# Gate weights loaded ahead, square roots of both scan directions taken together, and the latents' squares moved from PSUM to SBUF

## The chip, the cores and the metric

One core of a Trainium2 chip runs the whole program. The metric is the device time of one execution in microseconds; less is better. In the text, PE is the matrix engine, DVE the vector engine, ACT the scalar engine, POOL the GpSimd engine and SP the queue from which all transfers are issued.

## The reference, cut to what matters

One encoder layer on 1024 tokens of width 1024, in float32. The part that the change touches is the first sub-layer, before attention:

```python
proj = rms_norm(x, attn_norm) @ w_in          # [x-branch 512 | gate branch 512 | latents 416]
for d in (forward, backward):
    xd = depthwise_conv(xr, conv_w[d], conv_b[d])         # four taps
    r = sigmoid(block_diag(xd, w_a[d]) + b_a[d])
    i = sigmoid(block_diag(xd, w_i[d]) + b_i[d])
    log_a = -8 * r * softplus(-lam[d]);  a = exp(log_a)
    h[d] = scan(a, sqrt(-expm1(2 * log_a)) * (i * xd))    # h_t = a_t h_(t-1) + b_t
lru_out = (h[0] + h[1]) * gelu(yg)
c_q, c_kv = rms_norm(latents[:256]), rms_norm(latents[256:384])
```

Latent attention (8 heads), an output projection, a cross-attention into 256 memory rows and a SwiGLU network with a width-3 convolution follow; they are written as before.

## The kernel before

The kernel is one straight program without loops at run time. A scheduler builds the order of each engine's instructions from the program's order and from its own estimate of times; each engine then runs its list in that order and waits where an operand or a buffer isn't ready. So an instruction that waits holds back everything behind it on the same engine.

Activations are kept as two parts, high and low, so that each product of the projections is three matmuls (`mm3`, issued in `mm`, L108). The weights are split in the same way by POOL: `whi` (L133) and `wlo` (L134), from a raw tile with two buffers into tiles of a pool with 12 buffers.

The first sub-layer works on four blocks `j` of 128 channels:

- `xr_stage(j)` projects the x-branch into a two-bank PSUM tile `psin` (48 matmuls), ACT writes the first tap for each direction (L347), and DVE adds three taps for each direction out of PSUM (L349, L351), into `xf`. The PSUM tile is free after the last tap. There are two such two-bank tiles (`pb2`), which `psin`, `y_stage` and `latents` take in turn.
- `y_stage(j)` projects the gate branch (48 matmuls) and computes its GeLU: Square and Tanh on ACT (L358, L360), two steps on DVE (L359, L361), the last of which frees the PSUM tile.
- `lru_stage(j)` does, for each direction, four gate matmuls `psg` into one-bank tiles (`pb1`, four of them), Tanh of them on ACT into `thr` and `thi` (L380), Exp into `av` (L383), Tanh and Sqrt of `thr` (L384, L385), on DVE `(av+1)*thr` (L387) and `(thi+1)*xf` (L388), their product on POOL (L389; on DVE in the last block) and the scan on DVE (L392 forward, L394 backward). Then the directions are added (L396) and gated (L398). Sqrt is in another function table of ACT than Exp and Tanh, so that the scheduler's list has ACT_TABLE_LOAD before and after it.

`latents(t)` projects the 416 latent columns for 128 tokens into another two-bank tile `pslat` (24 matmuls), ACT copies them out (L421) and sums their squares (L424, L425). The squares themselves are of no use; they are written into the unused second bank of `pslat`. POOL and DVE then scale the rows (L426 to L429), PE transposes them (`psc`, L615), and the products `pk` and `pq` follow. `mem_rows` squares the memory rows (L598) and transposes them (`psm`, L605).

`rope_tables` uses a tile `rtt` with the tag "yt" and one buffer, the same as that of `y_stage`; its two Sin (L479, L480) need a third function table. `gate_unit` clears a weight tile on POOL and loads it with eight small transfers; `addrows` loads the parameter rows that become the columns `pcols`.

Of the kernel before, what the change touches and what calls it, by code (L numbers as in the profile page):

```python
# [11 lines left out]
F32 = mybir.dt.float32  # L12
F32R = mybir.dt.float32r
I32 = mybir.dt.int32
AF = mybir.ActivationFunctionType
ALU = mybir.AluOpType
# [3 lines left out]
S = 1024  # L20
D = 1024
P = 128
# [3 lines left out]
NJ = LRU // P  # L26
# [6 lines left out]
QL = 256  # L33
# [50 lines left out]
def trunk_layer(ctx: ExitStack, tc: tile.TileContext, a: dict, out: bass.AP):  # L84
    nc = tc.nc
    act, dve, pool, pe = nc.scalar, nc.vector, nc.gpsimd, nc.tensor
# [7 lines left out]
    wp = abcd.enter_context(tc.tile_pool(name="wp", bufs=12, reuse_waits="tile"))  # L94
# [9 lines left out]
    def f(t):  # L104
        return t.bitcast(F32)

    def mm(ps, l, r, start, stop):
        return pe.matmul(ps, lhsT=l, rhs=r, start=start, stop=stop)  # L108

    def mm3(ps, lh, ll, rh, rl, start, stop):  # L110
        mm(ps, lh, rh, start, False)
        mm(ps, lh, rl, False, False)
        return mm(ps, ll, rh, False, stop)
# [48 lines left out]
    tp = ab.enter_context(tc.tile_pool(name="tp", bufs=2, reuse_waits="tile"))  # L162
# [4 lines left out]
    for t in range(NT):  # L167
        xt = tp.tile([P, D], F32, tag=("xf", "xf", "th0", "th0", "th1", "th1", "th1", "a")[t],
                     bufs=4 if 4 <= t < 7 else 2, name="xt")
# [11 lines left out]
    for t in range(NT):  # L181
# [10 lines left out]
        h, o = t // 4, (t % 4) * P  # L192
        for q in range(2):
            ps = pb1.tile([P, 512], F32, tag="b1", name="psx")
# [4 lines left out]
            act.activation(hT[h][0][:, q * 4:q * 4 + 4, o:o + P], pv, AF.Copy)  # L199
            last_lo = dve.tensor_sub(hT[h][1][:, q * 4:q * 4 + 4, o:o + P], pv, f(hT[h][0])[:, q * 4:q * 4 + 4, o:o + P])  # L200


    RR = tp.tile([P, 6, P], F32, tag="xr", bufs=2, name="RR")
    R1, R2, R3 = RR[:, 0], RR[:, 1], RR[:, 2]
# [89 lines left out]
    sp2 = const.tile([P, 8], F32, name="sp2")  # L294
# [14 lines left out]
        return ps  # L309

    lru = lrup.tile([P, NJ, S], F32, tag="lru", name="lru")
    wg = {}

    def gate_unit(jj):

        w = wp.tile([P, 1024], F32, tag="w", name="wgate")
        pool.memset(w, 0.0)
        rv = w.rearrange("p (j d g c) -> p j d g c", j=2, d=2, g=2)
        for b in range(2):
            for gi, nm in enumerate(("lru_w_a", "lru_w_i")):  # L320
                for d in range(2):
                    nc.sync.dma_start(
                        rv[64 * b:64 * b + 64, :, d, gi, 64 * b:64 * b + 64],
                        a[nm][0, d].rearrange("(j b) p c -> b p j c", b=2)[b][:, 2 * jj:2 * jj + 2, :])
        wg[jj] = w

    ssl = const.tile([P, NT], F32, name="ssl")
    ssm = const.tile([P, NT], F32, name="ssm")
    krss = bc.tile([P, NT], F32, name="krss")
# [11 lines left out]
    def xr_stage(j):  # L341

        ps = in_proj(j * P)
        xfs = [tp.tile([P, S], F32, tag=("xf", "xr")[j % 2], bufs=2, name="xf") for _ in range(2)]
        cw = [[col("conv_w", (d * 4 + k) * 4 + j) for k in range(4)] for d in range(2)]
        for d in range(2):
            act.activation(xfs[d], ps, AF.Identity, bias=col("conv_b", d * 4 + j), scale=cw[d][3 - 3 * d])  # L347
        for n in range(1, 4):
            dve.scalar_tensor_tensor(xfs[0][:, n:], ps[:, :S - n], cw[0][3 - n], xfs[0][:, n:], ALU.mult, ALU.add)  # L349
        for n in range(1, 4):  # L350
            dve.scalar_tensor_tensor(xfs[1][:, :S - n], ps[:, n:], cw[1][n], xfs[1][:, :S - n], ALU.mult, ALU.add)  # L351
        return xfs
# [8 lines left out]
        dve.scalar_tensor_tensor(y, t, 1.0, ps, ALU.add, ALU.mult)  # L361

    def lru_stage(j, xfs):
        hs = []
        for d in range(2):
            i = d * 4 + j
            xf = xfs[d]
            pss = []
            for h in range(2):
                for g in range(2):  # L370
                    ps = pb1.tile([P, 512], F32, tag="b1", name="psg")
                    wo = ((j % 2) * 4 + d * 2 + g) * P
                    sl = slice(h * 512, (h + 1) * 512)
                    mm(ps, wg[j // 2][:, wo:wo + P], xf[:, sl], True, True)
                    pss.append(ps)
            thr = tp.tile([P, S], F32, tag="th0", name="thr")
            thi = tp.tile([P, S], F32, tag="th1", bufs=4, name="thi")
            for h in range(2):
                for g in range(2):
                    act.activation((thr, thi)[g][:, h * 512:(h + 1) * 512], pss[h * 2 + g], AF.Tanh,  # L380
                                   bias=hb[:, g * 8 + i:g * 8 + i + 1], scale=0.5)
            av = tp.tile([P, S], F32, tag="a", name="av")
            act.activation(av, thr, AF.Exp, bias=sp4[:, 8 + i:9 + i], scale=sp4[:, 8 + i:9 + i])  # L383
            act.activation(thr, thr, AF.Tanh, bias=sp2[:, i:i + 1], scale=sp2[:, i:i + 1])  # L384
            act.activation(thr, thr, AF.Sqrt, scale=0.25)  # L385
            m = thr
            dve.scalar_tensor_tensor(m, av, 1.0, thr, ALU.add, ALU.mult)  # L387
            dve.scalar_tensor_tensor(thi, thi, 1.0, xf, ALU.add, ALU.mult)  # L388
            (dve if j == NJ - 1 else pool).tensor_mul(thi, thi, m)  # L389
            h = thi  # L390
            if d == 0:
                dve.tensor_tensor_scan(h, av, thi, 0.0, ALU.mult, ALU.add)  # L392
            else:
                dve.tensor_tensor_scan(h[:, ::-1], av[:, ::-1], thi[:, ::-1], 0.0, ALU.mult, ALU.add)  # L394
            hs.append(h)
        dve.tensor_add(hs[0], hs[0], hs[1])  # L396
        y = lru[:, j, :]
        dve.scalar_tensor_tensor(y, hs[0], 0.5, y, ALU.mult, ALU.mult)  # L398
# [10 lines left out]

    cns = sm.tile([P, NT, LAT], F32, tag="cns", bufs=1, name="cns")  # L410

    def latents(t):
        h, o = t // 4, (t % 4) * P
        ps = pb2.tile([P, S], F32, tag="b2", name="pslat")
        for k in range(KD):
            wh, wl = wl_[k // 2]
            c = (k % 2) * LAT
            mm3(ps[:, :LAT], hT[h][0][:, k, o:o + P], hT[h][1][:, k, o:o + P],
                wh[:, c:c + LAT], wl[:, c:c + LAT], k == 0, k == KD - 1)
        cn = cns[:, t]  # L420
        act.activation(cn, ps[:, :LAT], AF.Copy)  # L421
        s2 = sm.tile([P, 2], F32, tag="s2", name="s2")
        junk = ps[:, 512:512 + QL]
        act.activation(junk, cn[:, :QL], AF.Square, scale=QL ** -0.5, accum_out=s2[:, 0:1])  # L424
        act.activation(junk[:, :KVL], cn[:, QL:QL + KVL], AF.Square, scale=KVL ** -0.5, accum_out=s2[:, 1:2])  # L425
        pool.tensor_scalar(s2, s2, EPS, 1.0, ALU.add, ALU.mult)  # L426
        pool.tensor_tensor(s2, s2, nhalf[:, :2], ALU.pow)
        dve.tensor_scalar(cn[:, :QL], cn[:, :QL], s2[:, 0:1], None, ALU.mult)
        dve.tensor_scalar(cn[:, QL:QL + KVL], cn[:, QL:QL + KVL], s2[:, 1:2], None, ALU.mult)  # L429
# [72 lines left out]

    xrs = {0: xr_stage(0)}
    xrs[1] = xr_stage(1)
    gate_unit(0)
    rC, rS = rope_tables()
    y_stage(0)
    lru_stage(0, xrs[0])
    xrs[2] = xr_stage(2)
    y_stage(1)  # L510
    gate_unit(1)
    lru_stage(1, xrs[1])
    xrs[3] = xr_stage(3)
    y_stage(2)
    lru_stage(2, xrs[2])
    y_stage(3)
    lru_stage(3, xrs[3])
    lat_units()
    for t in range(NT):
        latents(t)  # L520
# [293 lines left out]
    for s in range(NQ + 2):  # L814
        H, i = divmod(s, NT)
# [45 lines left out]
    def w_out_unit(half, kk):  # L861
        g = "lru_g" if kk < 2 else "mla_g"
        return wunit(lambda raw: pairs(raw, a["w_out"][0, kk * 2 * P:(kk + 1) * 2 * P, half * 512:(half + 1) * 512]),
                     1024, [col(g, (kk % 2) * 2), col(g, (kk % 2) * 2 + 1)], "ad")
# [66 lines left out]
    wo = [w_out_unit(0, kk) for kk in range(2)]  # L931
# [11 lines left out]
    with tc.issue_after(x2_load.ins):  # L943
        wo = [w_out_unit(1, kk) for kk in range(4)]
# [265 lines left out]
```

## Time and profile before

| | us |
|---|---|
| median of 3 runs | 1464.61 (1464.01 to 1468.86) |
| the profiled execution | 1464.37 |
| its span | 1462.3 |
| outside the span | 2.07 |
| PE busy in the span | 1405.3 (96%) |
| DVE, POOL, ACT busy | 866.1, 570.4, 545.8 |
| mean granted clock of PE | 0.993 |

All times in the text are microseconds from the start of the span. Busy time of PE includes pipelined overlap, so the idle rows of its list say more than its share. The first sub-layer up to the latents takes the first 206 us of the span; the network at the end takes about half of it, and PE has nearly no idle time there.

### The profile page before, as it was taken

Reading aid. Unit: us, or ns where it says so; the run is one execution under the profiler, and the core shown is the slowest. Engines: PE = TensorE matmul, PEld = TensorE weight load, DVE = VectorE, ACT = ScalarE, POOL = GpSimd, SP = SyncE. Lnnn points to the kernel's source line nnn. Section 1 sums busy time; section 2 is a strip of 40 time slices with the busy share of each in tenths; the row PEclk is TensorE's granted clock in tenths of the full one; section 3 lists DMA queues with packets and bytes.
Section 4 is the critical chain, followed back from the end, with each engine's and each line's share of the span. In section 5 each row is a group of like instructions: output and inputs, shape, how many; then the busy total and the mean of one; then the engine's idle time right before and its main releaser. Section 6 shows DMA issues by size and latency. Waiting matters only on the chain.

```text
span 1462.3 us, 17808 instructions
## 1 busy us (share of the span) xinstructions
PE 1405.3 (96%) x6964; PEld 1176.7 (80%) x6964; DVE 866.1 (59%) x1254; ACT 545.8 (37%) x900; POOL 570.4 (39%) x586
## 2 busy tenths in 40 slices
PE   6889899998999999999999999999999999999998
PEld 5657698787888888888878888888888888888887
DVE  6886847899998764676543443534343443534335
ACT  5465945687888731555222010111102010111110
POOL 7753644457697510111362332231423323231310
PEclk9999999999999999999999999999999999999999
DMA  5311101100000330201121121110202111120202
GB/s 194 82 35 37 43 30 44 58 1 2 1 1 1 109 122 30 58 1 43 30 73 58 42 60 43 44 58 30 59 28 72 44 57 44 43 58 29 58 0 115
DMA packets 72034, 70.92 MB, mean 48 GB/s; under 512 B 4858, under 2 KB 59407, under 8 KB 71951
## 3 DMA queue, kind: packets, MB, share of 16 engines
q1 hardware_dynamic: 71951, 69.78, 15.5%
q8 instruction: 55, 0.90, 0.3%
q14 instruction: 28, 0.23, 0.0%
HBM read 65.58 MB, written 4.19 MB: 48 GB/s over the span
## 4 chain that ended last, share of the span: by engine, by line
PE 78%; DVE 9%; ACT 7%; POOL 3%; issue 2%; DMA 1%; SPq 0%; ACTq 0%; DVEq 0%; POOLq 0%
PE psup L108 33%; PE psdn L108 16%; PE psP L108 6%; PE psS L108 3%; PE psq L108 3%; PE po L108 3%; PE psmo L108 3%; PE pslat L108 2%; PE psT L766 2%; DVE st L747 2%; PE psin L108 2%; DVE pT L770 2%; PE pq L108 1%; PE pkv L108 1%; POOL wlo L134 1%
## 5 line engine op out<-in xcount | busy, mean ns | idle before, releaser
L108 PE MATMUL psup<-h,whi 128*128 128x512 f32 x1408 | 437.5, 389 | 1.1 <-DVE gu L1138 0.9
L108 PEld LDWEIGHTS psup<-h,whi 128*128 128x128 f32 x1408 | 264.1, 188 | 56.8 <-issue 1.2
L108 PE MATMUL psup<-h,wlo 128*128 128x512 f32 x704 | 273.9, 389 | 0.0
L133 POOL TENSOR_SCALAR whi<-raw 128x1024 fp32r<-128x1024 f32 (+2 forms) x80 | 88.9, 1112 | 457.5 <-PE psup L108 238.5
L1136 ACT ACTIVATE gu<-psup,fcw 128x1024 f32<-128x1024 f32 x44 | 53.6, 1218 | 421.7 <-PE psup L108 421.7
L1137 DVE SCALAR_TENSOR_TENSOR gu<-psup,fcw,gu 128x1023 f32<-128x1023 f32 x44 | 56.4, 1283 | 251.5 <-ACT gu L1136 251.5
L134 POOL TENSOR_TENSOR wlo<-raw,whi 128x1024 fp32r<-128x1024 f32 (+2 forms) x80 | 195.3, 2441 | 11.4 <-PE psin L108 5.4
L1167 DVE TENSOR_TENSOR x<-x,psdn 128x512 f32<-128x512 f32 x176 | 119.4, 685 | 103.9 <-PE psdn L108 103.3
L108 PEld LDWEIGHTS psup<-h,wlo 128*128 128x128 f32 x704 | 132.2, 188 | 27.4
L108 PE MATMUL psdn<-whi,al 128*128 128x512 f32 x336 | 130.7, 389 | 0.0
L108 PE MATMUL psdn<-wlo,ah 128*128 128x512 f32 x336 | 130.7, 389 | 0.0
L108 PE MATMUL psdn<-whi,ah 128*128 128x512 f32 x336 | 130.5, 389 | 0.1
L108 PE MATMUL psS<-kT,qT 96*128 96x512 f32 x384 | 103.9, 404 | 3.9 <-ACT pr L751 3.8
L108 PE MATMUL psin<-hT,whi 128*128 128x512 f32 (+1 forms) x288 | 86.8, 385 | 8.0 <-DVE xf L351 6.6
L753 POOL TENSOR_SCALAR pr<-pr,st 128x1024 f32<-128x1024 f32 x64 | 71.7, 1121 | 53.8 <-DVE st L752 33.0
L770 DVE TENSOR_TENSOR pT<-psT,pT 128x512 fp32r<-128x512 f32 x128 | 84.4, 678 | 5.9 <-ACT pT L769 5.7
L751 ACT ACTIVATE pr<-psS,st,rqk 128x1024 f32<-128x1024 f32 x64 | 77.2, 1207 | 17.4 <-DVE st L749 13.4
L747 DVE TENSOR_REDUCE st<-psS 128x1 f32<-128x1024 f32 x64 | 77.7, 1214 | 8.1 <-PE psS L108 8.0
L108 PEld LDWEIGHTS psS<-kT,qT 96*128 96x128 f32 x384 | 67.5, 189 | 17.7 <-ACT pr L751 6.2
L108 PE MATMUL po<-pT,vt 128*128 128x256 f32 x512 | 72.3, 287 | 3.5 <-DVE pT L770 3.2
L769 ACT ACTIVATE pT<-psT 128x512 fp32r<-128x512 f32 x128 | 71.0, 596 | 8.1 <-PE psT L766 7.6
L108 PEld LDWEIGHTS psdn<-whi,ah 128*128 128x128 f32 x336 | 63.0, 188 | 13.6 <-DVE x L1167 0.5
(300 smaller groups left out, 2536.0 us busy)
## 6 DMA issues: line engine op xcount, KB each, us to landing
raw<-in_w_up SPq DMA_DIRECT2D x44, 512.0 KB
raw<-in_w_down SPq DMA_DIRECT2D x22, 512.0 KB
xt<-in_x SPq DMA_DIRECT2D x8, 512.0 KB
raw<-in_w_in SPq DMA_DIRECT2D x8, 512.0 KB
raw<-in_w_mem_kv SPq DMA_DIRECT2D x8, 512.0 KB
raw<-in_w_out SPq DMA_DIRECT2D x8, 512.0 KB
x<-in_x SPq DMA_DIRECT2D x8, 512.0 KB
out<-x SPq DMA_DIRECT2D x7, 512.0 KB
```

The source lines that it names most:

```text
L108: return pe.matmul(ps, lhsT=l, rhs=r, start=start, stop=stop)
L133: pool.tensor_scalar(hi[:, sl], raw[:, sl], 1.0, 0.0, ALU.mult, ALU.add)
L134: pool.tensor_sub(lo[:, sl], raw[:, sl], f(hi)[:, sl])
L747: dve.tensor_reduce(st[:, 0:1], psS, AX.X, ALU.max, negate=True)
L751: act.activation(pr, psS, AF.Exp, bias=st[:, 1:2], scale=r, accum_out=st[:, 2:3])
L753: scaled[s] = pool.tensor_scalar(pr, pr, st[:, 3:4], 0.0, ALU.mult, ALU.add)
L766: pe.transpose(ps[:, i * P:(i + 1) * P], pr[:, (n * 4 + i) * P:(n * 4 + i + 1) * P], ident)
L769: act.activation(dh, pv, AF.Copy)
L770: dve.tensor_sub(pTs[s // 2][n][1][:, :, qi * P:(qi + 1) * P], pv, f(dh))
L1136: act.activation(g, ps, AF.Identity, bias=fcv[:, 3, jj:jj + 1], scale=fcv[:, 1, jj:jj + 1])
L1137: dve.scalar_tensor_tensor(g[:, 1:], ps[:, :S - 1], fcv[:, 0, jj:jj + 1], g[:, 1:], ALU.mult, ALU.add)
L1167: dve.tensor_add(xs, xs, ps)
```

## The change

Three edits. `gate_unit(0)` stands ahead of the parameter rows rather than behind the second x-branch stage. `latents` writes its squares to a tile in SBUF, allocated once with the tag "yt" (one buffer). `lru_stage` does the gates, Exp and Tanh of both directions, then both Sqrt in a row behind the last Tanh, then the products and scans of both.

```diff
+    gate_unit(0)
     RR = tp.tile([P, 6, P], F32, tag="xr", bufs=2, name="RR")
...
     def lru_stage(j, xfs):
-        hs = []
+        hs, avs, thrs = [], [], []
         for d in range(2):
...
             act.activation(av, thr, AF.Exp, bias=sp4[:, 8 + i:9 + i], scale=sp4[:, 8 + i:9 + i])
-            act.activation(thr, thr, AF.Tanh, bias=sp2[:, i:i + 1], scale=sp2[:, i:i + 1])
-            act.activation(thr, thr, AF.Sqrt, scale=0.25)
-            m = thr
-            dve.scalar_tensor_tensor(m, av, 1.0, thr, ALU.add, ALU.mult)
-            dve.scalar_tensor_tensor(thi, thi, 1.0, xf, ALU.add, ALU.mult)
-            (dve if j == NJ - 1 else pool).tensor_mul(thi, thi, m)
-            h = thi
+            last = act.activation(thr, thr, AF.Tanh, bias=sp2[:, i:i + 1], scale=sp2[:, i:i + 1])
+            dve.scalar_tensor_tensor(thi, thi, 1.0, xfs[d], ALU.add, ALU.mult)
+            hs.append(thi)
+            avs.append(av)
+            thrs.append(thr)
+        with tc.issue_after(last.ins):
+            for d in range(2):
+                act.activation(thrs[d], thrs[d], AF.Sqrt, scale=0.25)
+        for d in range(2):
+            h, av, m = hs[d], avs[d], thrs[d]
+            dve.scalar_tensor_tensor(m, av, 1.0, m, ALU.add, ALU.mult)
+            (dve if j == NJ - 1 else pool).tensor_mul(h, h, m)
...
     def latents(t):
...
-        junk = ps[:, 512:512 + QL]
+        if t == 0:
+            junks.append(tp.tile([P, S], F32, tag="yt", bufs=1, name="junk"))
+        junk = junks[0][:, :QL]
...
     xrs[1] = xr_stage(1)
-    gate_unit(0)
```

Line numbers behind the edits move by up to eight: of the changed kernel, the taps are L351 and L353, the steps of the gate branch L360 to L363, `(thi+1)*xf` L385, Sqrt L391, `(av+1)*thr` L394, the product L395, the scans L397 and L399, the sum L400, the gating L402, and the latents' copy and squares L427, L432 and L433.

The scheduler's lists differ from the start of the span to the first products `pk` and `pq`; behind them they are the same. Three places follow.

ACT in block 0, behind the four Tanh of the first direction's gates. `rtt` is the rope table, `av` the Exp, `yt` the gate branch. Before:

```order
L479 ACT_TABLE_LOAD
L479 ACTIVATE rtt<-rtt 128x128
L347 ACTIVATE xf<-psin,pcols 128x1024
L480 ACTIVATE rtt<-rtt 128x128
L383 ACT_TABLE_LOAD
L383 ACTIVATE av<-thr,sp_326 128x1024
L384 ACTIVATE thr<-thr,sp_356 128x1024
L385 ACT_TABLE_LOAD
L385 ACTIVATE thr<-thr 128x1024
L358 ACTIVATE yt<-psin 128x1024
```

The same place in the changed kernel:

```order
L487 ACT_TABLE_LOAD
L487 ACTIVATE rtt<-rtt 128x128
L349 ACTIVATE xf<-psin,pcols 128x1024
L383 ACT_TABLE_LOAD
L383 ACTIVATE av<-thr,sp_336 128x1024
L488 ACT_TABLE_LOAD
L488 ACTIVATE rtt<-rtt 128x128
L384 ACT_TABLE_LOAD
L384 ACTIVATE thr<-thr,sp_366 128x1024
L360 ACTIVATE yt<-psin 128x1024
```

The second Sin now stands behind the first Exp, with a table load more before it and one more after it; the first Sqrt is gone from here.

DVE in block 1, from the gate branch to the taps of block 3 (`thr` is the step with the root, `thi` from `av` the scan). Before, with the forward direction's scan already done ahead of these rows:

```order
L359 SCALAR_TENSOR_TENSOR yt<-yt,psin 128x1024
L361 SCALAR_TENSOR_TENSOR lru<-yt,psin 128x1024
L388 SCALAR_TENSOR_TENSOR thi<-thi,xf 128x1024
L387 SCALAR_TENSOR_TENSOR thr<-av,thr 128x1024
L394 SCALAR_TENSOR_TENSOR thi<-av,thi 128x1024
L396 TENSOR_TENSOR thi<-thi 128x1024
L398 SCALAR_TENSOR_TENSOR lru<-thi,lru 128x1024
L349 SCALAR_TENSOR_TENSOR xf<-psin,pcols,xf 128x1023
```

The same place in the changed kernel:

```order
L361 SCALAR_TENSOR_TENSOR yt<-yt,psin 128x1024
L385 SCALAR_TENSOR_TENSOR thi<-thi,xf 128x1024
L363 SCALAR_TENSOR_TENSOR lru<-yt,psin 128x1024
L394 SCALAR_TENSOR_TENSOR thr<-av,thr 128x1024 x2
L385 SCALAR_TENSOR_TENSOR thi<-thi,xf 128x1024
L397 SCALAR_TENSOR_TENSOR thi<-av,thi 128x1024
L399 SCALAR_TENSOR_TENSOR thi<-av,thi 128x1024
L400 TENSOR_TENSOR thi<-thi 128x1024
L402 SCALAR_TENSOR_TENSOR lru<-thi,lru 128x1024
L351 SCALAR_TENSOR_TENSOR xf<-psin,pcols,xf 128x1023
```

Both directions' scans now stand between the gate branch of block 1 and the taps of block 3.

PE at the end of the latents. Before, nine of the transposes `psc` and three of `psm` stood between the earlier latents; in the changed kernel all of them stand behind the last:

```order
L108 MATMUL pslat<-whi,hT_120 128x416
L622 MATMUL psc<-ident,cns 128x128 x9
L612 MATMUL psm<-ident,mr 128x128 x4
L108 MATMUL pk<-whi,chl 128x512
L108 MATMUL pk<-wlo,chl 128x512
```

So twelve transposes have moved from between the latents to behind them.

More of the change, by code (lines that the diff above doesn't have):

```diff
@@ L200, in trunk_layer, with gate_unit @@
             last_lo = dve.tensor_sub(hT[h][1][:, q * 4:q * 4 + 4, o:o + P], pv, f(hT[h][0])[:, q * 4:q * 4 + 4, o:o + P])
+    wg = {}
+    def gate_unit(jj):
+        w = wp.tile([P, 1024], F32, tag="w", name="wgate")
+        pool.memset(w, 0.0)
+        rv = w.rearrange("p (j d g c) -> p j d g c", j=2, d=2, g=2)
+        for b in range(2):
+            for gi, nm in enumerate(("lru_w_a", "lru_w_i")):
+                for d in range(2):
+                    nc.sync.dma_start(
+                        rv[64 * b:64 * b + 64, :, d, gi, 64 * b:64 * b + 64],
+                        a[nm][0, d].rearrange("(j b) p c -> b p j c", b=2)[b][:, 2 * jj:2 * jj + 2, :])
+        wg[jj] = w
+    gate_unit(0)
     RR = tp.tile([P, 6, P], F32, tag="xr", bufs=2, name="RR")
@@ L311, in trunk_layer @@
     lru = lrup.tile([P, NJ, S], F32, tag="lru", name="lru")
[L312 to L325, printed above, removed]
     ssl = const.tile([P, NT], F32, name="ssl")
@@ L363, in lru_stage @@
     def lru_stage(j, xfs):
-        hs = []
+        hs, avs, thrs = [], [], []
         for d in range(2):
             i = d * 4 + j
-            xf = xfs[d]
             pss = []
@@ L372, in lru_stage @@
                     wo = ((j % 2) * 4 + d * 2 + g) * P
-                    sl = slice(h * 512, (h + 1) * 512)
-                    mm(ps, wg[j // 2][:, wo:wo + P], xf[:, sl], True, True)
+                    mm(ps, wg[j // 2][:, wo:wo + P], xfs[d][:, h * 512:(h + 1) * 512], True, True)
                     pss.append(ps)
@@ L383, in lru_stage @@
             act.activation(av, thr, AF.Exp, bias=sp4[:, 8 + i:9 + i], scale=sp4[:, 8 + i:9 + i])
-            act.activation(thr, thr, AF.Tanh, bias=sp2[:, i:i + 1], scale=sp2[:, i:i + 1])
-            act.activation(thr, thr, AF.Sqrt, scale=0.25)
-            m = thr
-            dve.scalar_tensor_tensor(m, av, 1.0, thr, ALU.add, ALU.mult)
-            dve.scalar_tensor_tensor(thi, thi, 1.0, xf, ALU.add, ALU.mult)
-            (dve if j == NJ - 1 else pool).tensor_mul(thi, thi, m)
-            h = thi
+            last = act.activation(thr, thr, AF.Tanh, bias=sp2[:, i:i + 1], scale=sp2[:, i:i + 1])
[6 more added lines that the diff above has]
+                act.activation(thrs[d], thrs[d], AF.Sqrt, scale=0.25)
+        for d in range(2):
+            h, av, m = hs[d], avs[d], thrs[d]
+            dve.scalar_tensor_tensor(m, av, 1.0, m, ALU.add, ALU.mult)
+            (dve if j == NJ - 1 else pool).tensor_mul(h, h, m)
             if d == 0:
-                dve.tensor_tensor_scan(h, av, thi, 0.0, ALU.mult, ALU.add)
+                dve.tensor_tensor_scan(h, av, h, 0.0, ALU.mult, ALU.add)
             else:
-                dve.tensor_tensor_scan(h[:, ::-1], av[:, ::-1], thi[:, ::-1], 0.0, ALU.mult, ALU.add)
-            hs.append(h)
+                dve.tensor_tensor_scan(h[:, ::-1], av[:, ::-1], h[:, ::-1], 0.0, ALU.mult, ALU.add)
         dve.tensor_add(hs[0], hs[0], hs[1])
@@ L410, in trunk_layer @@
     cns = sm.tile([P, NT, LAT], F32, tag="cns", bufs=1, name="cns")
+    junks = []
     def latents(t):
```

## The prediction

> **What bounds the kernel now.** The page first: PE is busy for 96% of the span, so time can only be won where PE is idle or slow, or lost by making it wait. The lists differ up to the first `pk` and `pq`, so I read PE's waits there (what PE waited for: total, times, longest), then PE's own list at the long ones (start, duration, last the idle time and its releaser).
>
> ```profile
> PE psin L108 <- DVE xf L351: 6.6, 2, 5.2
> PE pslat L108 <- ACT pslat L425: 5.8, 1, 5.8
> PE psg L108 <- POOL RR L286: 4.7, 1, 4.7
> PE psc L615 <- DVE mT L609: 0.7, 1, 0.7
> 111.01 1.19 PE L108 MATMUL psin<-hT,whi 128*128 128x512 f32 x2 [5.19 <-DVE xf L351]
> 134.87 3.59 PE L108 MATMUL psg<-xf,wgate 128*128 128x512 f32 x8
> 174.59 0.72 PE L108 MATMUL pslat<-whi,hT 128*128 128x416 f32 x1 [5.78 <-ACT pslat L425]
> 174.59 7.30 PE pslat L108 x24
> 182.22 4.54 PE pslat L108 x24
> 187.09 4.54 PE pslat L108 x24
> 205.74 0.71 PE L605 MATMUL psm<-ident,mr 128*128 128x128 f32 x5
> ```
>
> Three waits make most of it. The first latents after the wait of 5.78 take 7.30 instead of 4.54: PE restarts slowly, which adds 2.76. Between 111.01 and 134.87 stand 96 matmuls at about 0.2275 each (0.39 and its overlap), 21.8, so that wait added 2.0 as well.
>
> What opens each gate is on DVE and POOL:
>
> ```profile
> 52.26 1.27 DVE L349 SCALAR_TENSOR_TENSOR xf<-psin,pcols,xf 128x1021 f32<-128x1021 f32 x1
> 53.44 0.20 POOL L286 TENSOR_TENSOR RR<-RR 128x8 f32<-128x8 f32 x1
> 78.94 1.27 DVE L351 SCALAR_TENSOR_TENSOR xf<-psin,pcols,xf 128x1021 f32<-128x1021 f32 x1
> 106.95 3.91 DVE L351 SCALAR_TENSOR_TENSOR xf<-psin,pcols,xf 128x1023 f32<-128x1023 f32 x3
> 119.05 1.23 DVE L387 SCALAR_TENSOR_TENSOR thr<-av,thr 128x1024 f32<-128x1024 f32 x1 [3.55 <-ACT thr L385]
> 122.77 2.29 DVE L394 TENSOR_TENSOR_SCAN thi<-av,thi 128x1024 f32<-128x1024 f32 x1 [2.50 <-POOL thi L389]
> 125.10 2.83 DVE L396 TENSOR_TENSOR thi<-thi 128x1024 f32<-128x1024 f32 x1
> 127.96 1.78 DVE L398 SCALAR_TENSOR_TENSOR lru<-thi,lru 128x1024 f32<-128x1024 f32 x1
> 129.67 3.90 DVE L349 SCALAR_TENSOR_TENSOR xf<-psin,pcols,xf 128x1023 f32<-128x1023 f32 x3
> 133.49 3.91 DVE L351 SCALAR_TENSOR_TENSOR xf<-psin,pcols,xf 128x1023 f32<-128x1023 f32 x3
> 161.66 1.19 DVE L361 SCALAR_TENSOR_TENSOR lru<-yt,psin 128x1024 f32<-128x1024 f32 x1
> 120.36 2.38 POOL L389 TENSOR_TENSOR thi<-thi,thr 128x1024 f32<-128x1024 f32 x1 [13.51 <-DVE thr L387]
> 124.07 2.77 POOL L134 TENSOR_TENSOR wlo<-raw,whi 128x832 fp32r<-128x832 f32 x1 [1.33 <-PE psin L108]
> 126.82 1.85 POOL L133 TENSOR_SCALAR whi<-raw 128x832 fp32r<-128x832 f32 x1
> 130.02 0.92 POOL L132 TENSOR_SCALAR raw<-raw,pcols 128x768 f32<-128x768 f32 x1 [1.35 <-DMA raw<-in_w_uq]
> 134.96 1.96 POOL L134 TENSOR_TENSOR wlo<-raw,whi 128x832 fp32r<-128x832 f32 x1 [4.02 <-PE psin L108]
> ```
>
> The reader should see two things. The second gate (111.01) opens when the last taps of block 2 end, 106.95 + 3.91 = 110.86. And DVE and POOL take turns: the sum L396 begins at 125.10 and ends at 127.93, just 1.1 after POOL's split ended at 126.84; POOL's next split, alone about 0.9, ends only after L396; then L398 in turn takes 1.78. So where DVE reads two operands from SBUF while POOL works, times add up: L387, L388, the scan, L396 and L398 against POOL's products and splits. The taps, which read PSUM, don't suffer.
>
> The Trainium skill, page "SBUF — State Buffer", section "SBUF: two separate sides", calls the port pair of the two engines an exclusive lock, held for a whole instruction. By it all of these turns are serial, as in the sum below; without it the rival of covered turns holds. The rows above agree with the page.
>
> **Part 1, gate weights earlier: 0 (-0.7 to +0.7).** The wait before the first gate products is put down to POOL's L286, but that ends at 53.64, too late for the 53.74 start, and no operand of the products comes from it; the third tap L349 ends at 53.53, and is. DVE's taps are the late ones, not the weights. Eight transfers move ahead of nine parameter and position rows and the next weights on SP, and one clear of 0.95 on POOL goes into an idle place:
>
> ```profile
> 33.31 1.36 SPq L322 DMA_DIRECT2D wgate<-in_lru_w_a  x2
> 23.37 9.43 SPq L154 DMA_DIRECT2D raw<-in_w_in  x2
> 32.33 0.95 POOL L317 MEMSET wgate<- 128x1024 f32 x1
> 39.46 0.27 PE L232 MATMUL ptp<-ident,RR 128*128 128x128 f32 x1
> 70.15 1.05 POOL L133 TENSOR_SCALAR whi<-raw 128x1024 fp32r<-128x1024 f32 x1 [7.63 <-PE psin L108]
> 71.28 2.35 POOL L134 TENSOR_TENSOR wlo<-raw,whi 128x1024 fp32r<-128x1024 f32 x1
> 63.74 0.31 ACT L479 ACTIVATE rtt<-rtt 128x128 f32<-128x128 f32 x1 [2.60 <-DVE rtt L475]
> L385 ACT ACT_TABLE_LOAD x8 | 10.3, 1283 | 0.1
> 117.95 1.06 ACT L385 ACTIVATE thr<-thr 128x1024 f32<-128x1024 f32 x1
> 140.00:176.00 36.00, 30.22 (x118) 22.32 (x117) 26.84 (x18) 35.71 (x45) 20.47 (x13) 0.96 0.20 59
> ```
>
> Eight issues of about 0.65 make 5.3: the next weights are issued at 28.7 instead of 23.4, and POOL is free for them at about 32, so they may just be waited for. The parameter rows, issued by 27.8, are read by PE at 39.46. Weight splits move some us earlier, but PE doesn't wait for weights there. What is late next is still the taps.
>
> **Part 2, both roots together.** Eight loads of 1.283 before Sqrt become five and the loads back fewer too; one pair is added around the second Sin. The work that waits is what costs:
>
> *First gate (block 2 may start): 0, or -2.* The second Sin moves from 65.3 to 69.2 (Exp 1.24 and two loads more). DVE, with the cosine products behind it, stands from 66.5 to 69.5, then meets POOL's two splits of 70.15 to 73.6, and ends block 1's taps at about 80.0, where they ended before at 80.2 (78.94 + 1.27); if the small products slip in between the splits, at 77.7. I take half, -1.0, at the end.
>
> *Second gate (before 111.01): -2.0.* Block 0's first root ends at 84.6 (Tanh of the gate branch 78.7, then 1.2 of Exp, 1.2 of two gate Tanh, 1.2, 1.28, 1.06). From there, taking turns: two L394 2.4, two products 4.7, two scans 4.5, one split whi and wlo 0.9 + 1.96, L400 and L402 2.3: 16.8, to 101.4. The taps take 7.7 (3.90 + 3.91 less overlap): 109.1.
>
> *Third gate (`psin` of the last gate branch; before, PE came to it by itself at 134.87 + 3.0 = 137.9, the taps at 137.4): +5.2.* The root of block 1 comes 8.2 behind the second gate, as before (117.95 + 1.06 less 110.86). But the forward scan of block 1, done before the gate until now, lies behind it: two L394 2.4, two products 4.7, L385 1.2, two scans 4.5, split 2.9, L400 and L402 2.3, together 18.0; taps 7.7. So 8.2 + 18.0 + 7.7 = 33.9 instead of 26.5, and 109.1 + 33.9 = 143.0. PE waits some 7 here.
>
> *Fourth gate (the second `pslat`, whose PSUM tile is freed by the last step of block 3's gate branch, L363, which stands behind both scans of block 2): +10.3.* Before, it began 4.54 before PE's idle time from 168.8, at 164.3. Now: the root 14.6 behind the third gate (the fourth gate product of PE 9.9, then Exp, two Tanh, a load and the root), two L394 2.4, two products 4.7, two scans 4.5, splits of 768 columns 2.7, L385 1.2, L363 1.2, hand-overs 0.3: 31.6, at 174.6.
>
> **Part 3, squares in SBUF: -7.6.** From the second latents to the end of the last took 41.4 (164.3 to 205.7): seven of 4.54, the wait 5.78, the slow start 2.76, 1.1 of transposes in between. The wait falls: the third latents need only ACT's copy L427, not the squares. Now 31.8, 0.6 of wait for that copy behind the last roots' loads, and 1.4 for a slow start after the new wait of about 4 at the fourth gate (half of 2.76; nearest row): 33.8. Squares to SBUF cost ACT nothing that counts there; they wait for the "yt" tile, free at the fourth gate.
>
> **Behind the latents: +0.6.** Twelve transposes at 0.11 ((187.09 - 182.22 - 4.54) / 3) now stand there, 1.3; the wait of 0.74 falls. From `pkv` on the lists are the same and the shift goes through to the end.
>
> **Sum.** 10.3 - 7.6 + 0.6 = +3.3, less 1.0 for the first gate: +2.3 on the profiled 1464.37 (its span and 2.07 around it; the median is 0.24 above) gives 1466.7. The bounds: the splits may fall outside the turns (2.9 + 2.9 + 2.7 = 8.5 less), or POOL's scalings L132 (0.92 and about 1.05) come into them (2.0 more), the slow start may be 0 or 2.76 (-1.4 to +1.4), the first gate -1 to +1 of what I took, part 1 as above.
>
> **Rivals.**
>
> *Covered turns, faster.* DVE gets its operations in while POOL is between instructions, so the three splits cost nothing: 2.3 - 8.5 = -6.2, 1458.2. For it: POOL is busy for only 20.47 of the 36 us from 140 to 176 (the fifth number of the windows' row). Against it: L396's 2.83 and L398's 1.78.
>
> *ACT as the bound, faster.* From 140 to 176 ACT is busy for 35.71 of 36 (fourth number). If that sets the end, four loads fewer over all (19 against 15 in the lists) give 4 x 1.283 = 5.1: 1459.3. Against it: in the new order ACT waits for scans to free `av`. The Trainium skill, page "ScalarE: Activation LUTs", section "Table sets: the hidden batching unit", advises to group calls by table set; at the 2.7 us per switch that it states, an estimate by that page is 10.8 less, 1453.6. The trace has 1.283.
>
> *One POOL turn more, slower.* In block 1 before, L132 began at 130.02, after L398's end at 129.74: a transfer set that. In the new order its raw buffer may fill before the later L402, and L132 gets a turn in blocks 1 and 2: 0.95 + 1.05. PE's wait at the fourth gate is then over 5, like that of 5.78, with the full 2.76 rather than 1.4, and the first gate isn't early (1.0): +4.4 on the sum, 1471.1. It decides once the transfer lands before L402 starts.
>
> *No effect:* the gate weights do nothing, as part 1 has it; that is in the sum.
>
> **How the numbers follow.** The forecast has 0.55, with a range of its own from 1461.5 to 1470.5; covered turns 0.17; ACT 0.06; one POOL turn more 0.20; 0.02 elsewhere. A measurement tells about 0.3% from no change, 4.4 us, so 1460.2 to 1469.0 is the same. Faster takes the first two rivals, 0.23; slower the third and 0.11 of the forecast, with the rest 0.32; same 0.45. The range from 1457 to 1472 reaches past covered turns below and one POOL turn more above.
>
> **What would show it.** In the profile after: the wait of `pslat` for ACT's L433 gone (part 3 right); first gate products still near 53.7 (part 1); taps of block 3 ending near 143 with PE idle 5 to 8 ahead of the last `psin` (third gate); the second `pslat` waiting for DVE's L363, near 175. If the taps of block 3 end before 138, the turns were covered and I am wrong on the fast side; if lists behind `pkv` shift otherwise than the start of `pkv` does, the last step is wrong.

## The result, and the profile after

| | us |
|---|---|
| before, 14 runs | 1468.71 median (1463.52 to 1474.53) |
| changed, 14 runs | 1479.70 median (1473.85 to 1484.10) |
| ratio | 1.0076, 95% interval 1.0054 to 1.0098 |
| the changed kernel's profiled execution | 1484.10, span 1482.0, mean granted clock of PE 0.985 |

The change makes the kernel slower by some 11 us (0.0076 of 1468.71), where 2.3 were forecast (1466.7, and at most 1472). The profiled execution is the longest of its 14 runs, so what lies behind its first products `pk` is read with care below.

What PE waited for in the changed kernel, up to the first keys (total, times, longest):

```profile
PE psg L108 <- DVE RR L298: 10.0, 1, 10.0
PE psin L108 <- DVE xf L353: 10.0, 3, 5.8
PE pslat L108 <- DVE lru L363: 3.9, 1, 3.9
PE pslat L108 <- ACT cns L427: 2.3, 1, 2.3
```

The wait of 5.8 for ACT's squares is gone. The wait before the first gate products has grown from 4.7 to 10.0, and three waits are new: one of 5.8 before `psin` and the two before `pslat`. PE's own list places them (start, duration, last the idle time and its releaser):

```profile
58.33 6.46 PE L108 MATMUL psg<-xf,wgate 128*128 128x512 f32 x8 [10.03 <-DVE RR L298]
85.61 0.70 PE L108 MATMUL psin<-hT,whi 128*128 128x512 f32 x2 [1.51 <-DVE xf L353]
113.72 0.70 PE L108 MATMUL psin<-hT,whi 128*128 128x512 f32 x2 [2.63 <-DVE xf L353]
147.47 1.19 PE L108 MATMUL psin<-hT,whi 128*128 128x512 f32 x2 [5.82 <-DVE xf L353]
179.86 0.56 PE L108 MATMUL pslat<-whi,hT 128*128 128x416 f32 x1 [3.91 <-DVE lru L363]
188.49 0.46 PE L108 MATMUL pslat<-whi,hT 128*128 128x416 f32 x1 [2.29 <-ACT cns L427]
217.14 0.48 PE L108 MATMUL pk<-whi,chl 128*128 128x512 f32 x1
```

Against the rows of before, the first gate products are 4.59 later (53.74), the first gate 5.25 (80.36), the second 2.71 (111.01), the third 9.6 (137.9). The first keys `pk`, at 206.42 before, are 10.7 later. The remaining 9.0 of this execution's 19.7 arise behind them, in the attention stage.

What holds the first gate products is on POOL and DVE. POOL's list in the changed kernel:

```profile
35.06 1.06 POOL L133 TENSOR_SCALAR whi<-raw 128x1024 fp32r<-128x1024 f32 x1 [2.54 <-DMA raw<-in_w_in]
42.74 1.06 POOL L133 TENSOR_SCALAR whi<-raw 128x1024 fp32r<-128x1024 f32 x1 [0.65 <-DMA raw<-in_w_in]
44.20 0.20 POOL L293 TENSOR_SCALAR RR<-pcols 128x8 f32<-128x8 f32 x1
44.97 2.43 POOL L134 TENSOR_TENSOR wlo<-raw,whi 128x1024 fp32r<-128x1024 f32 x1
51.48 2.44 POOL L134 TENSOR_TENSOR wlo<-raw,whi 128x1024 fp32r<-128x1024 f32 x1
```

DVE's list at the same place (L460 and L466 belong to the rotation tables, L351 is the first tap):

```profile
44.44 0.17 DVE L294 TENSOR_TENSOR RR<-RR,pcols 128x8 f32<-128x8 f32 x1 [1.94 <-POOL RR L293]
45.06 3.38 DVE L460 TENSOR_SCALAR rtt<-rtt 128x128 f32<-128x128 f32 x2
51.43 2.64 DVE L466 SCALAR_TENSOR_TENSOR rtt<-rtt 128x128 f32<-128x128 f32 x2
53.99 1.27 DVE L351 SCALAR_TENSOR_TENSOR xf<-psin,pcols,xf 128x1023 f32<-128x1023 f32 x1
```

The raw weights come late, POOL waits 2.54 and 0.65 for them, and a split now stands ahead of the small parameter operations, which run at 44.20 instead of 41.12. DVE waits for the small one. Then two pairs of table operations, 0.36 and 0.60 long elsewhere in the list, take 3.38 and 2.64: the first ends behind POOL's `wlo` and the clear that follows it (47.4 and 48.3), the second behind the next `wlo` (53.9). The taps come behind them, at 53.99 instead of 48.01. The same place before:

```profile
41.12 0.20 POOL L276 TENSOR_SCALAR RR<-pcols 128x8 f32<-128x8 f32 x1
41.64 0.16 DVE L277 TENSOR_TENSOR RR<-RR,pcols 128x8 f32<-128x8 f32 x1
42.25 0.36 DVE L452 TENSOR_SCALAR rtt<-rtt 128x128 f32<-128x128 f32 x2
45.39 2.37 DVE L458 SCALAR_TENSOR_TENSOR rtt<-rtt 128x128 f32<-128x128 f32 x1
48.01 1.28 DVE L349 SCALAR_TENSOR_TENSOR xf<-psin,pcols,xf 128x1023 f32<-128x1023 f32 x1
```

There the first pair took 0.36, and only the first operation of the second pair lost a turn (2.37). So of the 6.0 by which the taps come later, 2.8 are there at the small operation (44.44 against 41.64), and 3.0 are the turn that the first pair now loses.

### The profile page after: what moved, and what is told of

The parts are those of the page before. It is cut to its first block, busy times and chain, and to the rows that moved or that the text cites. A ratio compares the mean times of both kernels' runs of the same rounds, so it can differ in the third digit from the quotient of the medians.

```text
span 1482.0 us, 17797 instructions
## 1 busy us (share of the span) xinstructions
PE 1412.5 (95%) x6964; PEld 1183.6 (80%) x6964; DVE 874.5 (59%) x1254; ACT 541.4 (37%) x896; POOL 579.1 (39%) x586
## 4 chain that ended last, share of the span: by engine, by line
PE 76%; DVE 10%; ACT 4%; POOL 2%; issue 2%; DMA 0%; DVEq 0%; ACTq 0%; POOLq 0%; SPq 0%
PE psup L108 32%; PE psdn L108 16%; PE psP L108 6%; PE psS L108 3%; PE po L108 3%; PE psq L108 3%; PE psmo L108 3%; PE psT L773 2%; DVE st L754 1%; PE pslat L108 1%; DVE pT L777 1%; POOL thi L395 1%; PE pq L108 1%; PE pkv L108 1%; PE psn L912 1%
## 5 line engine op out<-in xcount | busy, mean ns | idle before, releaser
L108 PE MATMUL psin<-hT,whi 128*128 128x512 f32 (+1 forms) x288 | 88.8, 392 | 11.2 <-DVE xf L353 10.0
L754 DVE TENSOR_REDUCE st<-psS 128x1 f32<-128x1024 f32 x64 | 77.7, 1215 | 12.5 <-PE psS L108 12.3
L108 PE MATMUL po<-pT,vt 128*128 128x256 f32 x512 | 75.8, 296 | 7.9 <-DVE pT L777 7.7
L108 PEld LDWEIGHTS po<-pT,vt 128*128 128x128 f32 x512 | 68.2, 198 | 11.0 <-DVE pT L777 5.1
L108 PEld LDWEIGHTS psin<-hT,whi 128*128 128x128 f32 x288 | 54.9, 199 | 25.1 <-issue 14.0
```

Source lines behind the costliest of these rows:

```text
L754: dve.tensor_reduce(st[:, 0:1], psS, AX.X, ALU.max, negate=True)
```

## Experiments

Each was timed in five rounds beside the kernel before; microseconds are the ratio's excess times the median of before in the same set (1464.88, 1466.86, 1468.60, 1466.84 and 1468.42 for the five sets).

| run | ratio (95%) | us on before |
|---|---|---|
| e1 gate weights first alone | 1.0036 (1.0022 to 1.0049) | +5.3 |
| e2 both roots alone | 1.0066 (1.0044 to 1.0088) | +9.7 |
| e3 squares in SBUF alone | 0.9965 (0.9950 to 0.9980) | -5.1 |
| e4 roots and squares | 1.0033 (1.0018 to 1.0049) | +4.8 |
| e5 e1, small operations first | 1.0058 (1.0042 to 1.0074) | +8.5 |
| e6 e1, gate weights on ACT's queue | 1.0038 (1.0020 to 1.0055) | +5.6 |
| e7 e2, products on DVE | 0.9973 (0.9958 to 0.9989) | -4.0 |
| e8 e3, tables later | 0.9947 (0.9930 to 0.9965) | -7.8 |
| e9 before, eight more transfers | 1.0003 (0.9986 to 1.0020) | +0.4 |
| e10 before, products on DVE | 1.0023 (1.0004 to 1.0041) | +3.4 |
| e11 e8, products on DVE | 0.9927 (0.9906 to 0.9948) | -10.7 |
| e12 e4, tables later, products on DVE | 0.9931 (0.9905 to 0.9958) | -10.1 |
| e13 changed, tables later | 0.9968 (0.9957 to 0.9979) | -4.7 |
| e14 e4, tables later | 0.9972 (0.9961 to 0.9984) | -4.1 |
| e15 changed, tables later, products on DVE | 0.9926 (0.9900 to 0.9952) | -10.9 |
| e16 changed, products on DVE | 1.0017 (1.0006 to 1.0028) | +2.5 |
| e17 e13, four more transfers | 0.9970 (0.9954 to 0.9986) | -4.4 |
| e18 e1, third weights early | 1.0023 (1.0002 to 1.0044) | +3.4 |

### The three parts, one at a time (e1 to e4)

Edits: the diff's hunk on `gate_unit(0)` alone (e1), on `lru_stage` alone (e2), on `junk` alone (e3), the last two together (e4).

> The kernel before with only the gate weights loaded ahead of the parameter columns. Queue theory (mine now): the eight transfers hold up SP's list by 5.3 us, POOL waits for raw weights (2.54 and 0.65 in the changed kernel), its small parameter operations come 3.3 later, DVE's taps come into POOL's splits: the first gate products start at 58 instead of 53.7 and the second gate follows, so the whole kernel is 4 to 6 us slower than before (ratio 1.003 to 1.004). Rival (the prediction's part 1): the loss at the first gate products is taken up before the last latents, 0 +- 1.5 us.

> The kernel before with only both directions' square roots taken together. Turns theory: third gate +6.9 and fourth gate +6.0 as in the changed kernel's profile, second gate -2.5: 8 to 12 us slower than before, with the second latents starting near 174.6 (the figure of the prediction). Rival (gate weights are the main loss, the roots only follow from them): less than 5 us slower, second latents before 169.

> The kernel before with only the latents' squares written to SBUF. Theory: the wait of 5.78 before the third latents and most of the slow restart (2.76) go: 4 to 8 us faster than before, last latents ending near 199. Rival (the wait changes its name): the third latents wait as long for ACT's copy or for another tile, and the time is within 2 us of before.

> The changed kernel with the gate weights loaded where they were before (roots and squares alone changed). Queue theory: 4 to 6 us faster than the changed kernel, so about +5 on before, first gate products near 53.7 again, first gate of block 2 near 80. Rival (the roots carry the whole loss, the gate weights only shift where PE waits): +9 to +11 on before, as the changed kernel.

Within their intervals the parts add up: 5.3 + 9.7 - 5.1 = 9.9, against some 11 for the whole. In e1 the first gate products start at 58.25; in e4 at 56.77, not near 53.7 as expected, which is told below. PE's list in e2 at the second, third and fourth gate:

```profile
109.25 0.70 PE L108 MATMUL psin<-hT,whi 128*128 128x512 f32 x2 [3.07 <-DVE xf L351]
142.34 1.19 PE L108 MATMUL psin<-hT,whi 128*128 128x512 f32 x2 [6.02 <-DVE xf L351]
174.76 0.53 PE L108 MATMUL pslat<-whi,hT 128*128 128x416 f32 x1 [3.92 <-DVE lru L361]
```

Forecast were 109.1, 143.0 and 174.6. In e3 the third latents wait 1.89 for ACT's copy where they waited 5.78 for the squares, so the rival of a wait that only changes its name falls too. The roots and the gate weights lose, the squares win.

### The products on DVE (e7, e10, e16)

```diff
-            (dve if j == NJ - 1 else pool).tensor_mul(h, h, m)
+            dve.tensor_mul(h, h, m)
```

> Both roots together alone (+9.7 us on before when measured), with the products of gate and root (thi by the root) on DVE in all four blocks instead of on POOL in the first three. If DVE and POOL take strict turns: a pair takes 2.4 of DVE instead of 4.7 in turn, 2.3 less at each of the second, third and fourth gate: 5 to 7 us faster than the roots alone, +3 to +5 on before. If POOL's products mostly ran beside DVE's other work: DVE has 2.4 more in each block and the kernel is 2 to 7 us slower than the roots alone, +12 to +17 on before.

> The kernel before, roots one at a time, with the products of gate and root on DVE in all blocks. If the products on POOL are what makes pairing dear (each takes a turn, and in pairs both are behind the last root): 0 to 5 us faster than before, and pairing with the products on DVE (3 us faster than before when measured) is worth 0 +- 3 us. If pairing costs as such (the forward scan behind the gate): 5 to 12 us faster than before, so that pairing costs 3 to 9 us of it.

> The changed kernel with the products on DVE in all blocks and nothing else. If POOL's products carry the loss of the paired roots: as much faster as they made the roots alone (13 us), so 0 to -5 us on before, with the gate weights' +5 and the squares' -5 still in it. If the DVE products only helped because the first gate fell early in that run's profile (53.84 against 56.75): 5 to 8 us faster than the changed kernel, +3 to +6 us on before.

The paired roots lose through POOL's products. PE's list of e7:

```profile
104.52 0.70 PE L108 MATMUL psin<-hT,whi 128*128 128x512 f32 x2 [2.02 <-DVE xf L351]
135.99 1.19 PE L108 MATMUL psin<-hT,whi 128*128 128x512 f32 x2 [6.00 <-DVE xf L351]
167.75 0.42 PE L108 MATMUL pslat<-whi,hT 128*128 128x416 f32 x1 [2.94 <-DVE lru L361]
```

The fourth gate comes 7.0 earlier than in e2. Of these, 2.9 stand there at the first gate products already (53.84 against 56.75, for a reason told below), and 4.1 are the saved turns, where 6.9 were expected of three gates. The third latents then wait 4.4 instead of 6.8, and `pk` starts 10.1 earlier (209.04 against 219.12). The times in the table differ by 13.7. In the whole change (e16 against the changed kernel) `pk` starts 5.8 earlier, 211.35 against 217.14, and the times by some 8.7 (11.2 and 2.5), which misses both ends of what was expected of e16. Where the 3 us or so between `pk` and the times come from is not settled.

In the old order (e10) the same edit gains nothing: the second gate comes 0.9 earlier (110.12), but PE then waits longer for ACT's squares, which stand behind the last block's Exp and Tanh in ACT's list. What PE waited for in e10:

```profile
PE pslat L108 <- ACT pslat L425: 8.6, 1, 8.6
```

Before it was 5.8. The profiled execution is the fastest of e10's 12 (1464.88, with a median of 1471.59), so it doesn't show where the +3.4 arises. With the products on DVE pairing isn't dear but worth 7.4 us (-4.0 against +3.4), which neither theory of e10 had. ACT loads a table 13 times in e7 and 19 times in e10; six loads of 1.28 are 7.7. That these are the gain, where ACT sets the end, is likely and not shown: e12 saves the same six against e11 (12 and 18), and gains nothing that can be measured.

### Why the gate weights cost (e5, e6, e9)

e5: POOL's fourth split tied behind the small operations.

```diff
+        elif c0 == LRU + P:
+            raw = w_in_load(c0)
+            with tc.issue_after(root.ins):
+                hi, lo = wsplit(raw)
```

e6: `(nc.scalar if jj == 0 else nc.sync).dma_start(` for the gate weights. e9: the kernel before with the same eight transfers into a tile `dummy`, ahead of the rows.

> The gate weights first alone (+5.3 us on before when measured), with POOL's weight split of the second gate branch held behind the small parameter operations, as POOL's list had it before; SP's order stays that of the gate weights first. If the late transfers alone are the cause: still +4 to +6 us on before. If the loss needs POOL to wait for a late transfer with the small operations queued behind it: the small operations run as soon as the parameter columns are there (39 instead of 43.8), first gate products at 53 to 57, 0 to +2.5 us on before.

> The gate weights first alone, but their first eight transfers issued from ScalarE's queue, so that SP's list isn't held up; POOL's list keeps the order of the gate weights first (the split ahead of the small operations). If the late transfers are the cause, alone or with the order: POOL's waits for raw weights (2.95 and 0.40) go, the small operations start near 41, first gate products at 53 to 57, 0 to +2.5 us on before. If POOL's order alone is the cause: still +4 to +6 us.

> The kernel before, with eight transfers of the gate weights' shape, into a tile that nothing reads, put on SP's list where the change puts the gate weights; the real ones stay where they were, and POOL's list keeps its order word for word. If SP's lateness is the cause of the loss at the first gate: raw weights come 5.3 us later, POOL's splits end 1.4 to 2 later, its small operations run at 42.3 or later instead of 41.0, first gate products at 56 to 60, +3 to +8 us on before. If it takes the clear and the split at their new places in POOL's list: 0 to +2 us.

Neither theory of e5 came through, e6 doesn't decide, and e9 came out in time as its second theory had it. e5 did not recover: the small operations ran at 42.52, but a pair of the tables' operations then lost a turn to the next split (DVE's list):

```profile
51.10 2.86 DVE L464 SCALAR_TENSOR_TENSOR rtt<-rtt 128x128 f32<-128x128 f32 x2
```

and the first gate products were at 59.46. e6 is no answer, though its time is the one expected of POOL's order alone, since ACT itself stood still for 6.88 from 12.5 on, with the first transfers in its list, and the first gate products came at 63.19. In e9 SP's lateness alone, with POOL waiting 1.35 for raw weights (2.95 and 0.40 in e1), cost nothing that can be measured.

But e9's profile shows the first gate products at 56.75 with POOL's old list, and so do e2 and e4 (56.75 and 56.77) and e3 (56.55), whose lists don't differ from that of before up to there; e7 and e10 have 53.84 and 53.73. The stretch from 34 to 37 us tells them apart (busy time of each engine; the last three numbers are PE's granted clock, the share of the DMA engines and GB/s). Before, then e9:

```profile
34.00:37.00 3.00, 3.00 (x18) 2.61 (x19) 2.75 (x5) 1.09 (x2) 2.92 (x2) 1.00 0.70 191
```

```profile
34.00:37.00 3.00, 3.00 (x13) 2.61 (x14) 2.69 (x5) 1.20 (x2) 2.35 (x2) 0.59 0.75 200
```

Behind an idle time of 2.15 PE's clock is granted at 1.00 in one execution and at 0.59 in another (0.50 to 0.67 in e2, e3, e4 and e11; 1.00 in e7, e8, e10 and e12). In the nine profiles where that idle time is 1.25 or 1.26, those with the gate weights first on SP's queue and e14, it is 1.00 each time. Behind the low clock the parameter columns come 1.3 to 1.5 later, and a table operation of DVE misses its place ahead of a POOL split, in e9:

```profile
46.61 3.20 DVE L461 TENSOR_SCALAR rtt<-rtt 128x128 f32<-128x128 f32 x1
```

so that the first taps start at 51.12 instead of 48.01, and `pk` at 210.82 instead of 206.42. The runs of before lie around 1464.4 and 1469, 4.5 apart; that these are the two starts fits, but only one execution of before was profiled (1464.37, with the clock at 1.00). So the gate weights first cost 7.3 at `pk` (213.76 in e1) against the start of before's profile, and 2.9 against that of e9's. The taps start at 48, 51.1 or, in e1, e5 and the changed kernel, 54: some 3 us, about one turn behind POOL, between each two. The Trainium skill, page "TensorE: Matmul & The Clock Gate", section "Part 1: The HAM clock gate", says of a kernel's start that the activity window is free-running, so that the same kernel runs a different number of matmuls cold from run to run. The rows show the like behind an idle time at 34 us; that the phase of a window makes it, no run here shows. It puts the penalty under 1% of a span and advises not to fit it; here it was 4.4 us at `pk` in e9 (0.3%), because turns hang on it.

### The tables out of the way (e8, e11 to e15, e17, e18)

```diff
-    rC, rS = rope_tables()
     y_stage(0)
...
+    rC, rS = rope_tables()
     lat_units()
```

with the squares' tile under the tag "th0". e17 adds four of the transfers of e9 to e13. e18 is e1 with `w_third = w_in_load(LRU)` behind `w_second`.

> Squares in SBUF (3.4 to 5 us faster than before when measured) and the rotation tables computed behind the last recurrence block instead of ahead of the first. Theory: DVE's taps of block 0, whose input is there at 44.6, no longer stand behind the tables' small operations; first gate products 3 to 5 us earlier, 7 to 13 us faster than before in all. Rival: the tables' 10 us of DVE and two table loads of ScalarE only move to the latents and hold up the keys and queries there: within 2 us of the squares alone, 2 to 6 us faster than before.

> The changed kernel with the rotation tables behind the last recurrence block. If the gate weights' loss comes about because the tables' DVE operations, ahead of block 0's taps, lose one more turn to a POOL split: no such operations are left there, first gate products at 50 to 52.5, and the kernel is within 0 to +1.5 us of the next run's. If it is the late weights or the small parameter operations (43.95 instead of 41.0) that set the first gate by themselves: first gate products 3 to 5 us later than in the next run, and 3 to 6 us slower than it.

> Roots and squares changed, gate weights where they were, tables behind the last block: the partner of the run before. Both theories: first gate products near 50, some 3 to 6 us faster than with the tables ahead (which was +4.9 us on before when measured): -2 to +2 us on before.

> The changed kernel with the tables later (3 to 5 us faster than before when measured) and four more transfers of the gate weights' shape on SP's list, into a tile that nothing reads, so that the raw weights come 2.6 us later than there (they weren't late there: POOL did not wait for them). If late raw weights set the first gate by themselves: POOL waits 2 to 3 for them again, first gate products at 52 to 55, 3 to 5 us slower than without the transfers. If they only do harm by pushing POOL's splits into the tables' operations: first gate products at 49 to 51 all the same, within 1.5 us.

> The gate weights first alone, with the third weight load put on SP's list ahead of them all but one; POOL's list is word for word that of the gate weights first alone (+5.3 us on before when measured). If late raw weights start the loss: POOL's wait of 2.95 goes, its small operations run near 41, the taps start at 48 to 51 as in the kernel before, 0 to +2.5 us on before. If POOL's order (clear and split at new places) makes it: first gate products at 58 still, +4 to +6 us.

With the tables behind the last block, the gate weights first cost nothing measurable (e13 against e14, -4.7 and -4.1). In e13 the raw weights came in time, though. e17 makes them late again, as late as in the changed kernel. POOL's list of e17:

```profile
35.48 1.05 POOL L133 TENSOR_SCALAR whi<-raw 128x1024 fp32r<-128x1024 f32 x1 [2.92 <-DMA raw<-in_w_in]
44.34 0.20 POOL L300 TENSOR_SCALAR RR<-pcols 128x8 f32<-128x8 f32 x1
```

and PE's:

```profile
49.08 3.67 PE L108 MATMUL psg<-xf,wgate 128*128 128x512 f32 x8 [0.74 <-DVE xf L358]
```

The same lateness, the same late small operation, and the first gate products start at 49.08 (48.90 in e13). The time is the same within the intervals (-4.4 and -4.7), though `pk` of this execution is 2.3 later than e13's (206.43 and 204.09). e18 has the tables in place and the weights in time. DVE's list of e18, where POOL has a `wlo` from 42.55 to 44.99, the clear to 45.89, and the next `wlo` from 49.08 to 51.52:

```profile
42.64 3.39 DVE L455 TENSOR_SCALAR rtt<-rtt 128x128 f32<-128x128 f32 x2
49.03 2.64 DVE L461 SCALAR_TENSOR_TENSOR rtt<-rtt 128x128 f32<-128x128 f32 x2
```

Both turns are lost as in the changed kernel, and the first gate products are at 55.93, 2.3 earlier than in e1; the kernel is at +3.4 (0.3 to 6.4) instead of +5.3. It fell between the two expectations. So the loss needs the tables' operations ahead of the taps. Of the lateness at the first gate products the late weights make 2.3 in these profiles, and POOL's new order is enough for the rest; the times of e1 and e18, whose intervals overlap, don't separate the two.

> Squares in SBUF, tables behind the last block (8 to 10 us faster than before when measured) and the products on DVE, roots one at a time. If the products take turns on the path: 2 to 6 us faster than without them on DVE, 10 to 15 faster than before. If PE's wait at the second gate is set by ScalarE's root (118.96 in the profile before) and not by the product: within 2 us of the tables later, 7 to 11 faster than before.

> As the run before it, with both directions' roots together. If pairing costs as such, 3 to 9 us slower than the run before it; if only POOL's products made it dear, within 3 us of it, and 10 to 16 us faster than the kernel before.

> The whole change with the tables later and the products of gate and root on DVE. Turns of the tables' operations as the cause of the gate weights' loss: within 1.5 us of the same without the gate weights first (10 us faster than before when measured), -8 to -12 us on before. Late weights as the cause: 3 to 6 us slower than that, -4 to -8 us.

e8's first gate products start at 49.83, and it gains 7.8. e14 came out faster than either theory had it (-4.1, where -2 to +2 was expected): moving the tables is worth 2.7 beside e3, 8.9 beside e4 and 15.9 beside the changed kernel. e11, e12 and e15 beat both kernels, with medians of 1457.23, 1456.00 and 1454.34. Their intervals overlap, so neither the paired roots nor the gate weights first gain or cost anything measurable once tables and products no longer take turns with POOL's work.

## Why the prediction was wrong

**Part 1 failed: "What is late next is still the taps", 0 (-0.7 to +0.7).** Measured were +5.3 (3.2 to 7.2). That the taps are the late ones was right; that they stay where they were was not. The step asked whether PE waits for the weights, not who else waits for POOL while POOL waits for a transfer. The prediction had "they may just be waited for"; POOL waited 2.54, its small operations came 3.1 later, and DVE's tables lost one more turn of about 3.0 ahead of the taps. e17, beside e13 and e14, shows that without the tables there the same late weights and small operations cost nothing measurable; e18 shows that POOL's new order, without late weights, still costs the turn. A sign could be read in the profile before: the first three taps run from 48.01 to 53.53 though they are 3.9 of work, with table operations between them, one of which took 1.33.

**Part 2 came true in mechanism and size.** The first gate was put at 80.0 and came at 85.61, from part 1. From gate to gate the forecast was 29.1, 33.9 and 31.6; measured were 28.1, 33.75 and 32.4. From block 1's roots to the taps of block 3 the sum had 18.0, and DVE's list has 17.7 (121.90 to 139.60). The price in time of e2 alone, +9.7, stands against 10.3 less 1.0. The lock of the port pair that the prediction took from the Trainium skill, page "SBUF — State Buffer", section "SBUF: two separate sides", agrees with the rows shown here. What the prediction didn't ask is whether the products need be on POOL: e7 shows that the whole loss of the paired roots hangs on them.

**Part 3 was right, one term too small.** The wait for the squares went. From the second latents to `pk` 35.1 were forecast (33.8 and 1.3 of transposes) and 37.3 were measured (217.14 - 179.86): the copy is waited for 2.29 instead of 0.6, and the slow restart takes 1.8 (188.49 - 179.86 - 4.54 - 2.29) instead of 1.4. Alone (e3) the squares bring `pk` to 203.80, 7.0 ahead of e9's, whose first gate lies at the same place, and 5.1 are gained in time.

**The sum** at `pk` was 208.7 (206.42 and 2.3) and is 217.14. The 8.4 of difference are 4.6 at the second gate, 0.6 between there and the fourth, 2.2 of part 3, and the 1.0 taken off for an early first gate. Without part 1 the sum was near: e4's `pk` at 212.81 is 2.0 behind e9's with the same start, where +2.3 was forecast; its time is further off, at +4.8 (2.6 to 7.2).

**"From `pkv` on the lists are the same and the shift goes through to the end"** holds for the medians (some 11 against 10.7 at `pk`) and not for the profiled execution, where 9.0 were added, 7.9 of them between 280 and 503 of before's span. Over that stretch the shift changes by less than 0.5 in the profiles of e1, e2, e7, e9, e10 and e18, but grows by 1.5, 1.9 and 2.7 in those of e3, e4 and e16, so the step does not hold in each of them. The same row of DVE's list in the attention stage, before and then in the changed kernel:

```profile
413.94 1.13 DVE L559 TENSOR_SCALAR rqk<-rqk 128x8 f32<-128x8 f32 x1
```

```profile
428.93 4.60 DVE L566 TENSOR_SCALAR rqk<-rqk 128x8 f32<-128x8 f32 x1
```

POOL's instructions stand without a gap from 428.02 to 434.9, and DVE's tiny operation seems to have lost to several in a row; PE then waits 4.3 for `pT`, and its clock falls to 0.91 in that stretch. PE's waits of this kind add up to 7.7 in this execution and to 3.2 to 4.3 in those of before, e1 to e4 and e16. One more profile has the same row at that length: e8's, with 4.61 at 406.43 and a wait of 4.3 behind it. It took 1462.97, where five of e8's eight runs took 1456.7 to 1457.3. That such turns decide part of the spread of the kernels' runs is likely, not shown.

**The rivals.** Covered turns fell: 33.75 is the price with all turns. One POOL turn more was not it: PE's wait at the fourth gate is 3.91, not over 5. ACT as the bound, given 0.06, is what e10's longer wait for ACT points to in the old order, not in the new. What came, a later first gate through POOL's list, was none of them.

## What to carry to other kernels

A transfer that moves ahead on one queue delays the ones behind it, and the engine that waits for those delays its whole list: follow that list to whoever waits for its small operations, even where the moved data is not waited for by anyone. Where DVE operations with operands in SBUF stand ahead of critical work while another engine on the same ports works through a list without gaps, the cost came in whole instructions of that engine here, so move the uncritical ones (here the rotation tables, 2.7 to 15.9 us) away rather than shortening them. Before pairing work to save table loads, see which engine does what then stands behind the pair: the same pairing was 9.7 us slower with the products on POOL and 7.4 us better than no pairing with them on DVE, and of no measurable worth once the squares and the tables were moved too (e11 and e12).

## What had not been expected of the hardware

- A DVE operation that waits for the ports seems to lose against several POOL instructions in a row, not just the running one: 4.60 and 4.61 (e8), beside a POOL list without gaps, for one that took 1.13 in before.
- PE's granted clock behind the same idle time of 2.15 was 1.00 in five profiles and 0.50 to 0.67 in five others. With the tables ahead of the taps the first gate products came 2.8 to 3.0 later in the latter, and `pk` 4.4 later in e9.
- Eight transfers of 32 KB, read by nobody, on SP's queue cost nothing measurable (+0.4, -2.1 to +2.9) though they made POOL wait 1.35.
